# Strassen's scheme for the gate products of two feed-forward stages

## The chip, the core and the metric

The kernel runs on one core of a Trainium2 chip. The metric is the device time of one execution in microseconds (us). Engines: TensorE (PE; its weight loads are shown apart, as PEld), VectorE (DVE), ScalarE (ACT), GpSimd (POOL) and SyncE (SP, which here issues DMAs).

## What is computed

A sequence of 512 tokens with 1024 features goes through two blocks in float32: a convolution mixer and a dilated attention mixer, each with a gated projection behind it; then a feed-forward stage, a mixer (sparse attention and an mLSTM), and a second feed-forward stage. The change touches the two feed-forward stages alone:

```python
def swiglu_ffn(x, g, w_gate, w_up, w_down):   # x (1, 512, 1024), w_gate, w_up (1024, 2816), w_down (2816, 1024)
    h = rms_norm_2(x, g)
    return (jax.nn.silu(h @ w_gate) * (h @ w_up)) @ w_down
...
x = x + 0.5 * swiglu_ffn(x, ...)
```

## The kernel before

Activations lie transposed, features on the 128 partitions and the 512 tokens along the row: x is eight tiles of 128x512 (k.xT). All large products are made in three passes: each operand is split into a high part (rounded to the type fp32r, which TensorE takes) and a low part (the rest), and mm3 (line 216) issues high x high, high x low and low x high into one PSUM bank. Each of the three matmuls loads its own 128x128 weights.

Weights come through one stream (class Stream, line 54) in a fixed order of *granules*, mostly 512 KB, written down in weight_specs. load (line 64) issues a granule's DMA from SP into one of 4 raw buffers (RBUFS). split (line 73) makes the high part on ScalarE (line 85) and the low part on VectorE, or on GpSimd for granules whose number is in POOL_LO (line 87); both halves have 6 buffers (WBUFS). fill keeps six granules split ahead of the first that is still in use; done notes that a granule is used up and lets fill run a few ticks later (a tick is one call of mm3).

A feed-forward stage (ffn, line 1453) has 22 inner tiles of 128 features. For each, a_tile takes the gate granule ("fg") and the up granule ("fu"): eight blocks of 128 input features, 24 matmuls of 512 columns each, into one PSUM bank. The input is split without the norm's factor, so e1 multiplies gate and up by the factor nm.rB out of PSUM on VectorE, with silu on ScalarE between; e2 multiplies the two and splits the product. The first two tiles run as one group of four banks, and half-way through it the norm's statistics are made (Norm.stats, with a power on GpSimd, line 213). The down product is made in parts of 8, 8 and 6 inner tiles (FFN_PARTS): after the first tile of the next part, down (line 1481) runs eight output tiles over the part's inner tiles, and out adds each to k.xT (line 1489). ffn_order (line 430) writes this order, ffn_specs (line 443) the granules that it takes. Arena (line 116) hands out 71 tiles of SBUF and 8 PSUM banks.

The order of the work on each engine is the order of these calls, but for a scheduler that places instructions by its own estimate of when they can run; generators added by add_side are advanced a little at every tick.

Of the kernel before, what the change touches and what calls it, by code (L numbers as in the profile page):

```python
# [11 lines left out]
F32 = mybir.dt.float32  # L12
F32R = mybir.dt.float32r
I32 = mybir.dt.int32
AF = mybir.ActivationFunctionType
OP = mybir.AluOpType
# [7 lines left out]
GRAN = 1024  # L24
WBUFS = 6
FILL = 3
UNITS = ('aq', 'mx', 'mo', 'mv')
POOL_KEYS = ()
# [5 lines left out]
POOL_LO = (0, 1, 2, 3, 4, 5) + tuple(range(24, 37))  # L34
RBUFS = 4
# [9 lines left out]
def gran(key, w, k0, nk, *cols):  # L45

    pieces, off = [], 0
    for c0, n in cols:
        pieces.append((off, n, w[k0 * 128:(k0 + nk) * 128, c0:c0 + n].rearrange("(k p) c -> p k c", p=128)))
        off += n  # L50
    return key, nk, off, pieces


class Stream:
# [3 lines left out]
    def __init__(self, k, pool, specs):  # L58
        self.k, self.pool, self.specs = k, pool, specs
        self.raw, self.parts, self.held = {}, {}, set()  # L60
        self.nd = self.ns = self.pos = 0
        self.hold, self.due = False, None

    def load(self):
        i = self.nd
        self.nd += 1
        t = self.pool.tile([128, GRAN], F32, tag="raw", name="raw", bufs=RBUFS)
        _, nk, width, pieces = self.specs[i]
        for off, n, src in pieces:
            self.k.nc.sync.dma_start(t[:, :nk * width].rearrange("p (k c) -> p k c", k=nk)[:, :, off:off + n], src)  # L70
        self.raw[i] = t

    def split(self):
        i = self.ns
        while self.nd <= min(i + RBUFS - 1, len(self.specs) - 1):
            self.load()
        self.ns += 1
        n = self.specs[i][1] * self.specs[i][2]
        raw = self.raw.pop(i)
        hi = self.pool.tile([128, GRAN], F32R, tag="whi", name="whi", bufs=WBUFS)  # L80
        lo = self.pool.tile([128, GRAN], F32R, tag="wlo", name="wlo", bufs=WBUFS)
        with ExitStack() as ctx:
            if self.k.behind is not None:
                ctx.enter_context(self.k.tc.issue_after(self.k.behind.ins))
            self.last_hi = self.k.nc.scalar.activation(hi[:, :n], raw[:, :n], AF.Copy)  # L85
            eng = self.k.nc.gpsimd if i in POOL_LO or self.specs[i][0][0] in POOL_KEYS else self.k.nc.vector
            eng.tensor_tensor(lo[:, :n], raw[:, :n], hi[:, :n].bitcast(F32), OP.subtract)  # L87
        self.parts[i] = (hi, lo)

    def fill(self, limit=None):  # L90
        first = min(self.held) if self.held else self.pos
# [12 lines left out]
    def done(self, i):  # L104
        self.held.discard(i)
        self.parts.pop(i)
        if self.due is None:
            self.due = self.k.t + FILL
# [170 lines left out]
class Norm:  # L279
# [9 lines left out]
    def add(self, x):  # L289
        k, nc = self.k, self.k.nc  # L290
        hi, lo = k.mem.get(F32R), k.mem.get(F32R)
        g = k.col(self.gain, self.at + self.n)
        sq = k.mem.get()
        nc.scalar.activation(hi, x, AF.Copy, scale=g)
        nc.scalar.activation(sq, x, AF.Square)
        self.finish()
        self.open = (x, hi, lo, g, sq)
        self.n += 1
# [77 lines left out]
def weight_specs(a):  # L376
# [18 lines left out]
    for n in range(4):  # L395
        sp.append(gran(("ao", n), a["attn_w_out"][0], 0, 4, (256 * n, 256)))
    ple_specs(sp, a, 1)
    ffn_specs(sp, a, 1)
    w = a["w_in_2"][0]
    for n in range(4):  # L400
# [15 lines left out]
    for n in range(8):  # L416
        sp.append(gran(("wo", n), a["w_out_2"][0], 0, 8, (128 * n, 128)))
    ffn_specs(sp, a, 2)
    return sp

# [3 lines left out]
        sp.append(gran((key, j), w, 2 * j, 2, (c0, 512)))  # L424


FFN_PARTS = (8, 8, 6)


def ffn_order():  # L430

    order, k0 = [], 0
    for p, n in enumerate(FFN_PARTS):
        for i in range(n):
            order.append(("up", k0 + i))
            if p and i == 0:
                order.append(("down", p - 1))
        k0 += n
    order.append(("down", len(FFN_PARTS) - 1))
    return order  # L440


def ffn_specs(sp, a, l):
    wg, wu, wd = (a[f"ffn{l}_w_{n}_2"][0] for n in ("gate", "up", "down"))
    for what, i in ffn_order():
        if what == "up":
            sp.append(gran(("fg", l, i), wg, 0, 8, (128 * i, 128)))
            sp.append(gran(("fu", l, i), wu, 0, 8, (128 * i, 128)))
        else:
            for m in range(8):  # L450
                sp.append(gran(("fd", l, i, m), wd, sum(FFN_PARTS[:i]), FFN_PARTS[i], (128 * m, 128)))


def pp_specs(sp, a, l):
# [24 lines left out]
def vectors(k, load_x):  # L479
# [31 lines left out]
    def rest():  # L511
# [7 lines left out]
        k.mem.put(pr, dr)  # L519

    load(0, 1)
    load_x()
    for _ in range(3):
        k.W.load()
    dw = a["conv_dw"][0].rearrange("t (c f) -> (t c) f", f=128)
    nc.sync.dma_start(dr[:124, 0:128], dw[0:124])
    nc.sync.dma_start(dr[:124, 128:256], dw[124:248])
    load(1, len(parts))
    return first, rest

# [922 lines left out]
def ffn(k, l, nm, done):  # L1453

    nc, mem, ps_ = k.nc, k.mem, k.ps
    V = nc.vector
    X, H, T = nm.X, {}, {}
    order = ffn_order()
    starts = [sum(FFN_PARTS[:p]) for p in range(len(FFN_PARTS))]
    count = 0  # L1460
    queue = deque()

    def e1(i, pg, pu):
        a, b = mem.get(), mem.get()
        V.tensor_tensor(a, pg, nm.rB, OP.mult)  # L1465
        ps_.put(pg)
        nc.scalar.activation(a, a, AF.Silu)
        V.tensor_tensor(b, pu, nm.rB, OP.mult)  # L1468
        ps_.put(pu)
        queue.append((i, a, b))  # L1470
        while len(queue) > 1:
            e2()

    def e2():
        i, a, b = queue.popleft()
        V.tensor_tensor(a, a, b, OP.mult)  # L1476
        mem.put(b)
        H[i] = k.split_into(a)
        mem.put(a)

    def down(p):
        n, k0 = FFN_PARTS[p], starts[p]
        last = p == len(FFN_PARTS) - 1
        while queue and queue[0][0] < k0 + n:
            e2()
        Hs = [H.pop(k0 + i) for i in range(n)]

        def out(m, ps):
            V.scalar_tensor_tensor(k.xT[m], ps, 0.5, k.xT[m], OP.mult, OP.add)  # L1489
            ps_.put(ps)  # L1490
            if last:
                done(m)
        m0 = 0
        if last:
            m0 = 4
            pss = k.a_group(Hs, [("fd", l, p, m) for m in range(4)])
            for m in range(4):
                out(m, pss[m])
        for m in range(m0, 8):
            out(m, k.a_tile(Hs, ("fd", l, p, m)))  # L1500
        for h, lo in Hs:
            mem.put(h, lo)

    i = 0
    while i < len(order):
        what, j = order[i]
        if what == "down":
            if j == len(FFN_PARTS) - 1:
                for h, lo in nm.X:
                    mem.put(h, lo)  # L1510
            down(j)
        elif i == 0:
            p4 = k.a_group(X, [("fg", l, 0), ("fu", l, 0), ("fg", l, 1), ("fu", l, 1)], nm.stats)
            k.defer(0, lambda: e1(0, p4[0], p4[1]))
            k.defer(0, lambda: e1(1, p4[2], p4[3]))
            i += 1
        else:
            pg = k.a_tile(X, ("fg", l, j))
            pu = k.a_tile(X, ("fu", l, j))
            k.after(lambda j=j, pg=pg, pu=pu: e1(j, pg, pu))  # L1520
        i += 1
    mem.put(nm.rB)

# [532 lines left out]
@with_exitstack  # L2058
def body(ctx, tc, *args):
    a = dict(zip(_INS, args[:-1]))  # L2060
    k = Kern(ctx, tc, a, args[-1])
    k.W = Stream(k, k.wp, weight_specs(a))
    nm, pp = layer0(k)
    nm1 = Norm(k, "norm", 8, keep=True)
    ple(k, 0, nm, pp, nm1)
    nm, pp = layer1(k, nm1)
    nm3 = Norm(k, "ffn1")
    ple(k, 1, nm, pp, nm3)
    nm4 = Norm(k, "mix")
    ffn(k, 1, nm3, lambda m: nm4.add(k.xT[m]))  # L2070
    nm4.finish()
    nm5 = Norm(k, "ffn2")
    mixer(k, nm4, nm5)
    ffn(k, 2, nm5, store(k))
    k.flush()
# [27 lines left out]
```

## Time and profile before

| | |
|---|---|
| median of 3 runs | 1829.97 us (1829.23 to 1831.29) |
| profiled execution | 1830.0 us, span 1828.0 us, mean granted TensorE clock 0.991 |
| TensorE busy in the span | 1793.0 us (98%), 8316 matmuls |
| VectorE, ScalarE, GpSimd busy | 1074.1, 805.8, 257.1 us |
| mean DMA rate | 89 GB/s |

The span runs from the first to the last instruction. Matmuls are pipelined and their ends are modelled: the printed duration of one is longer than the step from its start to the next one's, and the step is what a sequence of them costs. L12 is line 12 of the kernel; tiles are named by their program names: b is a PSUM bank, s a tile of the arena, whi and wlo the weights' high and low parts, raw a granule as loaded.

### The profile page before, as it was taken

To read this page: it belongs to the slowest core of one execution; us is meant where nothing else is said; L and a number is where in the kernel's file an instruction comes from. 1 tells how busy PE (TensorE), PEld (TensorE's weight loads), DVE (VectorE), ACT (ScalarE), POOL (GpSimd) and SP (SyncE) were. 2 spreads that over 40 slices of the span, in tenths; PEclk is the share of its full clock that TensorE was granted. 3 is DMA by queue.
4 is the path that set the end of the run, shared out by engine and by line. 5 is a ranking of instruction groups with operands and counts; after the bars stand their busy time and mean duration, and the time that the engine had idled before them with its cause. 6 is when DMAs were issued, how large, how long until landed. Compare 5 with 4: busy or idle time off the path is not lost. (4 is left out here: it accounts for less than half of the span.)

```text
span 1828.0 us, 21884 instructions
## 1 busy us (share of the span) xinstructions
PE 1793.0 (98%) x8316; PEld 1459.3 (80%) x8316; DVE 1074.1 (59%) x2064; ACT 805.8 (44%) x1345; POOL 257.1 (14%) x210
## 2 busy tenths in 40 slices
PE   7998899999999999999999999899999999999999
PEld 6876688888888888888888887778888888888887
DVE  6989667755466665434433559997446554344342
ACT  6776535465556443222212436567632333122221
POOL 4999210302120000000000001000000000000000
PEclk9999899999999999999999999899999999999999
DMA  6322133212322233333332432013232333333321
GB/s 191 112 81 81 47 93 116 70 53 84 97 85 67 81 93 86 97 94 92 93 92 79 133 113 87 24 52 89 68 125 83 93 104 93 93 94 100 95 70 46
DMA packets 262484, 161.91 MB, mean 89 GB/s; under 512 B 10000, under 2 KB 244844, under 8 KB 262380
## 3 DMA queue, kind: packets, MB, share of 16 engines
q1 hardware_dynamic: 262380, 160.53, 30.2%
q8 instruction: 65, 1.06, 0.2%
q14 instruction: 39, 0.32, 0.1%
HBM read 155.23 MB, written 5.28 MB: 88 GB/s over the span
## 5 line engine op out<-in xcount | busy, mean ns | idle before, releaser
L219 PE MATMUL b<-s,whi 128*128 128x512 f32 x1856 | 740.9, 399 | 0.2
L218 PE MATMUL b<-s,whi 128*128 128x512 f32 x1856 | 737.8, 400 | 3.2 <-ACT s L563 2.2
L220 PE MATMUL b<-s,wlo 128*128 128x512 f32 x1856 | 738.8, 398 | 0.0
L85 ACT ACTIVATE whi<-raw 128x1024 fp32r<-128x1024 f32 (+2 forms) x288 | 297.4, 1041 | 683.1 <-PE b L219 440.9
L218 PEld LDWEIGHTS b<-s,whi 128*128 128x128 f32 x1856 | 350.4, 189 | 88.5 <-ACT s L563 2.6
L219 PEld LDWEIGHTS b<-s,whi 128*128 128x128 f32 x1856 | 351.0, 189 | 86.5 <-issue 2.4
L220 PEld LDWEIGHTS b<-s,wlo 128*128 128x128 f32 x1856 | 350.1, 189 | 83.1 <-issue 1.2
L87 DVE TENSOR_TENSOR wlo<-raw,whi 128x1024 fp32r<-128x1024 f32 (+2 forms) x269 | 331.1, 1234 | 57.2 <-ACT whi L85 50.7
L218 PE MATMUL b<-whi,s 128*128 128x512 f32 (+1 forms) x416 | 172.5, 416 | 0.2 <-DVE s L1772 0.2
L219 PE MATMUL b<-wlo,s 128*128 128x512 f32 (+1 forms) x416 | 168.9, 406 | 0.0
L220 PE MATMUL b<-whi,s 128*128 128x512 f32 (+1 forms) x416 | 165.1, 397 | 0.0
L642 POOL TENSOR_TENSOR s<-s,s 128x512 f32<-128x512 f32 x88 | 128.2, 1488 | 3.4 <-ACT s L638 2.2
L1489 DVE SCALAR_TENSOR_TENSOR s<-b,s 128x512 f32<-128x512 f32 x48 | 33.1, 691 | 144.7 <-PE b L220 144.6
L1468 DVE TENSOR_TENSOR s<-b,s 128x512 f32<-128x512 f32 x44 | 30.4, 691 | 138.4 <-PE b L220 138.4
L644 DVE SCALAR_TENSOR_TENSOR b<-s,s,b 128x512 f32<-128x512 f32 x144 | 99.9, 747 | 3.6 <-ACT b L632 2.9
L220 PEld LDWEIGHTS b<-whi,s 128*128 128x128 f32 x416 | 79.2, 190 | 13.8
L218 PEld LDWEIGHTS b<-whi,s 128*128 128x128 f32 x416 | 79.3, 191 | 12.7 <-DVE s L1772 0.3
L219 PEld LDWEIGHTS b<-wlo,s 128*128 128x128 f32 x416 | 79.3, 191 | 11.0
L1465 DVE TENSOR_TENSOR s<-b,s 128x512 f32<-128x512 f32 x44 | 30.4, 691 | 93.3 <-PE b L220 93.3
L638 ACT ACTIVATE s<-s,s 128x512 f32<-128x512 f32 x96 | 66.2, 717 | 35.0 <-POOL s L642 34.9
L213 POOL TENSOR_TENSOR h8y<-hv,mhalf 128x8 f32<-128x8 f32 x28 | 47.4, 1694 | 131.4 <-DVE hv L1001 113.9
L232 ACT ACTIVATE s<-s 128x512 fp32r<-128x512 f32 x56 | 35.3, 631 | 42.3 <-DVE s L1476 31.8
(417 smaller groups left out, 1698.9 us busy)
## 6 DMA issues: line engine op xcount, KB each, us to landing
raw<-in_ffn_w_gate SPq DMA_DIRECT2D x44, 512.0 KB
raw<-in_ffn_w_up SPq DMA_DIRECT2D x44, 512.0 KB
raw<-in_attn_w_in SPq DMA_DIRECT2D x40, 512.0 KB
raw<-in_w_in SPq DMA_DIRECT2D x36, 512.0 KB
raw<-in_ffn_w_down SPq DMA_DIRECT2D x32, 512.0 KB
raw<-in_conv_w_in SPq DMA_DIRECT2D x24, 512.0 KB
raw<-in_ple_w_gate SPq DMA_DIRECT2D x16, 512.0 KB
raw<-in_ffn_w_down SPq DMA_DIRECT2D x16, 384.0 KB
```

The costliest lines, as they stand in the source:

```text
L85: self.last_hi = self.k.nc.scalar.activation(hi[:, :n], raw[:, :n], AF.Copy)
L87: eng.tensor_tensor(lo[:, :n], raw[:, :n], hi[:, :n].bitcast(F32), OP.subtract)
L213: self.nc.gpsimd.tensor_tensor(y, v, self.mhalf[:, :shape], OP.pow)
L218: mm(ps, a[0], b[0], start=first, stop=False)
L219: mm(ps, a[0], b[1], start=False, stop=False)
L220: self.last = mm(ps, a[1], b[0], start=False, stop=last)
L232: i = nc.scalar.activation(hi, src, AF.Copy)
L638: k.tap = nc.scalar.activation(p, y[:, nd + sent:nd + sent + S], AF.Copy, scale=wcol(nd + sent, c))
L642: nc.gpsimd.tensor_tensor(acc2, acc2, p, OP.add)
L644: nc.vector.scalar_tensor_tensor(acc, y[:, t:t + S], wcol(t, c), acc, OP.mult, OP.add)
L1465: V.tensor_tensor(a, pg, nm.rB, OP.mult)
L1489: V.scalar_tensor_tensor(k.xT[m], ps, 0.5, k.xT[m], OP.mult, OP.add)
```

## The change

In each stage the first 6 inner tiles stay as they are (FFN_PLAIN), and the other 16 go in eight pairs. For a pair, the gate product is seen as a 2x2 block product: the weights of two inner tiles (two columns) by two halves of the 1024 input features (two rows), and the input by two halves of the features and two halves of the tokens. Strassen's scheme, in Winograd's form, makes it from seven products of half-size blocks instead of eight, with sums of blocks on both sides and combinations of the products.

- The input: turn_x, a side generator in the time of tiles 2 to 5, multiplies x by the norm's gain and factor, forms the sums t1 to t4 and splits blocks and sums; turn_rest makes the last eight splits inside the first pair. The result is 16 split tiles (TX) per stage, in place of nm.X.
- The weights: a pair takes four "fs" granules (split_sums): the first gate tile as it is; two sums; two sums; the rest of the second tile. Two are loaded, the other two are made of the same raw buffers, which stay in use longer. VectorE makes four sums of 512 columns per pair.
- The products (two): seven products of 4 blocks x 3 passes, each for 256 tokens, so 256 columns per matmul and two products to a bank. The up products of the pair take the same token halves, also in matmuls of 256 columns.
- The combinations: first, second and third add the products out of PSUM on VectorE in seven operations of 256 columns. The norm's factor is already in, so the multiplications by rB are gone for these tiles.
- FFN_PARTS becomes (6, 4, 6, 6), so the down product has four parts a stage and 64 granules in both stages instead of 48.
- The low parts of the gate and up granules from tile 2 on, of all down granules, and of the first and last "fs" granule of a pair move from VectorE to GpSimd (POOL_MORE, halves).

```diff
@@ class Stream
     def split(self):
         i = self.ns
-        while self.nd <= min(i + RBUFS - 1, len(self.specs) - 1):
+        while self.nd < len(self.specs) and (self.live < RBUFS or not self.specs[self.nd][3]):
             self.load()
...
+        if key[0] == "fs":
+            return self.split_sums(i, key[3])
...
+    def halves(self, parts, cols, src, pool=False):
+        hi, lo = (t[:, cols] for t in parts)
...
+            self.last_hi = self.k.nc.scalar.activation(hi, src, AF.Copy)
+            eng = self.k.nc.gpsimd if pool else self.k.nc.vector
+            eng.tensor_tensor(lo, src, hi.bitcast(F32), OP.subtract)
+
+    def split_sums(self, i, j):
+        V, mem = self.k.nc.vector, self.k.mem
+        one, two = slice(0, 512), slice(512, 1024)
+        p = self.parts[i] = self.two()
+        if j == 0:
+            A = self.blk["a"] = self.raw.pop(i)
+            self.halves(p, slice(0, 1024), A, True)
+        elif j == 1:
+            B = self.blk["b"] = self.raw.pop(i)
+            A = self.blk["a"]
+            s1, s2 = mem.get(), mem.get()
+            V.tensor_tensor(s1, B[:, one], B[:, two], OP.add)
+            V.tensor_tensor(s2, s1, A[:, one], OP.subtract)
+            self.halves(p, two, s2)
+            self.halves(p, one, s1)
...
+        elif j == 2:
+            A, B, s2 = self.blk.pop("a"), self.blk["b"], self.blk.pop("s")
+            s3 = mem.get()
+            V.tensor_tensor(s3, A[:, one], B[:, one], OP.subtract)
+            V.tensor_tensor(s2, A[:, two], s2, OP.subtract)
+            self.live -= 1
+            self.halves(p, one, s3)
+            self.halves(p, two, s2)
...
+        else:
+            self.halves(p, one, self.blk.pop("b")[:, two], True)
+            self.live -= 1
@@
-FFN_PARTS = (8, 8, 6)
+FFN_PARTS = (6, 4, 6, 6)
+FFN_PLAIN = 6
@@ def ffn_specs
+        elif what == "two":
+            for j in range(2):
+                sp.append(gran(("fs", l, i, j), wg, 0, 8, (128 * (i + j), 128)))
+            sp.append(gran(("fu", l, i), wu, 0, 8, (128 * i, 128)))
+            for j in (2, 3):
+                sp.append((("fs", l, i, j), 8, 128, []))
+            sp.append(gran(("fu", l, i + 1), wu, 0, 8, (128 * (i + 1), 128)))
...
+POOL_MORE = {(n, l, i) for n in ("fg", "fu") for l in (1, 2) for i in range(2, 22)}
+POOL_MORE |= {("fd", l, p, m) for l in (1, 2) for p in range(len(FFN_PARTS)) for m in range(8)}
@@ def ffn
+    def turn_x():
...
+        for j in range(2):
+            q = {}
+            for kh in range(2):
+                for th in range(2):
+                    t = q[kh, th] = mem.get()
+                    for e in range(2):
+                        n = 4 * kh + 2 * j + e
+                        V.scalar_tensor_tensor(t[:, e * 256:(e + 1) * 256], k.xT[n][:, th * 256:(th + 1) * 256],
+                                               k.col(nm.gain, nm.at + n), nm.rB[:, th * 256:(th + 1) * 256],
+                                               OP.mult, OP.mult)
...
+            V.tensor_tensor(t1, b12, b11, OP.subtract)
+            V.tensor_tensor(t2, b22, t1, OP.subtract)
...
+            for name, t in (("t2", t2), ("t1", t1)):
+                TX[name, j] = k.split_into(t)
...
+        def product(ps, th, e, off, name):
...
+            for kk in range(4):
+                c = slice(off + kk * 128, off + kk * 128 + 128)
+                b = [t[:, halves2[kk % 2]] for t in TX[name, kk // 2]]
+                k.mm3(ps[:, halves2[th]], (hi[:, c], lo[:, c]), b, kk == 0, kk == 3)
...
+        def plain(i):
...
+            for th in range(2):
+                for kk in range(8):
+                    b = [t[:, halves2[kk % 2]] for t in TX[("b11", "b12", "b21", "b22")[kk // 4 * 2 + th], kk % 4 // 2]]
+                    k.mm3(ps[:, halves2[th]], k.wpart(g, kk * 128), b, kk == 0, kk == 7)
...
+        product(x, 0, 0, 0, "b11")
+        product(x, 1, 0, 512, "b21")
+        k.W.done(gs[0])
+        if wait:
+            turn_rest()
+        product(y, 0, 1, 512, "t2")
+        product(y, 1, 1, 0, "t1")
+        k.W.done(gs[1])
+        def first():
+            nc.scalar.activation(p1, x[:, L], AF.Copy)
+            add(a0[:, L], x[:, R], p1)
+            ps_.put(x)
+            add(u2, y[:, L], p1)
+            add(u4, y[:, R], u2)
+        k.after(first)
+        pu0 = plain(i0)
+        z, w = ps_.get(), ps_.get()
+        product(z, 0, 2, 0, "t3")
+        product(z, 1, 2, 512, "b22")
+        k.W.done(gs[2])
+        def second():
+            add(a0[:, R], z[:, R], u4)
+            add(u3, z[:, L], u2)
+            add(a1[:, R], y[:, R], u3)
+            ps_.put(y, z)
+            nc.scalar.activation(a0, a0, AF.Silu)
+        k.after(second)
+        product(w, 0, 3, 0, "t4")
+        k.W.done(gs[3])
+        def third():
+            add(a1[:, L], u3, w[:, L], OP.subtract)
...
+            nc.scalar.activation(a1, a1, AF.Silu)
+            add(a0, a0, pu0, OP.mult)
+            ps_.put(pu0)
+            H[i0] = k.split_into(a0)
...
+        pu1 = plain(i0 + 1)
+        def end():
+            add(a1, a1, pu1, OP.mult)
+            ps_.put(pu1)
+            H[i0 + 1] = k.split_into(a1)
...
```

## Rows read from the trace of the kernel before

**Rows 1.** The page: busy time, share of the span and instructions of each engine.

```profile
PE 1793.0 (98%) x8316; PEld 1459.3 (80%) x8316; DVE 1074.1 (59%) x2064; ACT 805.8 (44%) x1345; POOL 257.1 (14%) x210
```

**Rows 2.** Windows of both stages: length; PE, PEld, DVE, ACT, POOL busy us; clock; DMA.

```profile
703.00:1072.00 369.00, 369.00 (x1586) 296.79 (x1585) 162.50 (x203) 103.78 (x128) 4.13 (x7) 1.00 0.35 100
1463.00:1826.00 363.00, 360.62 (x1573) 291.25 (x1571) 147.48 (x179) 95.84 (x116) 1.01 (x1) 1.00 0.30 87
```

**Rows 3.** Groups of TensorE, 700 to 1072 us: busy us, mean ns, idle before.

```profile
L218 PE MATMUL b<-s,whi 128*128 128x512 f32 x527 | 208.2, 395 | 0.0
```

**Rows 4.** Timeline of TensorE, 24 steps in each stage: start us, duration us.

```profile
906.06 0.39 PE L218 MATMUL b<-s,whi 128*128 128x512 f32 x1
...
911.69 0.39 PE L218 MATMUL b<-s,whi 128*128 128x512 f32 x1
...
1599.68 0.39 PE L218 MATMUL b<-s,whi 128*128 128x512 f32 x1
...
1605.26 0.39 PE L218 MATMUL b<-s,whi 128*128 128x512 f32 x1
```

**Rows 5.** Timeline of TensorE in the mixer, 1099.77 to 1105.59 us.

```profile
1099.77 0.39 PE L219 MATMUL b<-wlo,s 128*128 128x512 f32 x1
...
1102.80 0.39 PE L220 MATMUL b<-whi,s 128*128 128x512 f32 x1
1103.04 0.64 PE L984 MATMUL b<-s,s 128*128 128x256 f32 x4
1103.51 0.64 PE L985 MATMUL b<-s,s 128*128 128x256 f32 x4
1103.99 0.28 PE L984 MATMUL b<-s,s 128*128 128x256 f32 x1
1104.10 0.29 PE L985 MATMUL b<-s,s 128*128 128x256 f32 x1
...
1104.80 0.37 PE L984 MATMUL b<-s,s 128*128 128x256 f32 x1
1105.00 0.28 PE L985 MATMUL b<-s,s 128*128 128x256 f32 x1
...
1105.59 0.39 PE L218 MATMUL b<-whi,s 128*128 128x512 f32 x1
```

**Rows 6.** Timeline of TensorE, matmuls of 336 columns, 21 steps.

```profile
1086.72 0.31 PE L219 MATMUL b<-wlo,s 128*128 128x336 f32 x1
...
1089.94 0.32 PE L219 MATMUL b<-wlo,s 128*128 128x336 f32 x1
```

**Rows 7.** Groups of VectorE by shape, 760 to 1050 us (first stage).

```profile
L87 DVE TENSOR_TENSOR wlo<-raw,whi 128x1024 fp32r<-128x1024 f32 x45 | 55.0, 1223 | 5.7 <-ACT whi L85 5.7
L1476 DVE TENSOR_TENSOR s<-s,s 128x512 f32<-128x512 f32 x16 | 11.1, 691 | 1.4
```

**Rows 8.** Groups of GpSimd in the whole span: the low part of 1024 columns.

```profile
L87 POOL TENSOR_TENSOR wlo<-raw,whi 128x1024 fp32r<-128x1024 f32 x19 | 46.5, 2458 | 41.2 <-ACT whi L85 41.2
```

**Rows 9.** Groups of ScalarE by shape, 760 to 1050 us.

```profile
L85 ACT ACTIVATE whi<-raw 128x1024 fp32r<-128x1024 f32 x45 | 47.7, 1061 | 164.7 <-PE b L219 116.1 <-issue 48.6
L232 ACT ACTIVATE s<-s 128x512 fp32r<-128x512 f32 x16 | 10.1, 633 | 13.3 <-DVE s L1476 13.3
```

**Rows 10.** VectorE's subtraction, 42 to 140 us, and that window (columns as in rows 2).

```profile
L87 DVE TENSOR_TENSOR wlo<-raw,whi 128x1024 fp32r<-128x1024 f32 x18 | 31.2, 1732 | 6.6 <-ACT whi L85 5.7 <-POOL s L642 1.0
...
42.00:140.00 98.00, 97.31 (x414) 76.84 (x412) 90.11 (x110) 73.60 (x107) 97.14 (x65) 1.00 0.33 97
```

**Rows 11.** Timeline of SP's queue at the start: DMA issues.

```profile
4.97 5.48 SPq L70 DMA_DIRECT2D raw<-in_conv_w_in  x3
```

**Rows 12.** Timeline of ScalarE at the start: the first granules' high parts.

```profile
13.22 2.08 ACT L85 ACTIVATE whi<-raw 128x1024 fp32r<-128x1024 f32 x2
```

**Rows 13.** Line 218, 700 to 1072 us: events on the load queue (ns, min/median/max).

```profile
L218 PEldq EVENT_SEMAPHORE  x1: 51/51/51, 733.3 to 733.3; - x1
```

**Rows 14.** Timeline of weight loads for matmuls of one column, 1463 us.

```profile
1463.03 0.86 PEld L319 LDWEIGHTS b<-ones,s 128*128 128x128 f32 x7
```

## Prediction: what the change does to the time

> **What bounds the kernel now.** I read the page's engine totals first: TensorE is busy 1793.0 of the 1828.0 us span, VectorE 1074.1, ScalarE 805.8 and GpSimd 257.1 [rows 1]. That is an average over unlike stages, so I next cut out the two feed-forward stages by windows [rows 2]. Each is some 370 us long; TensorE fills 369.00 of 369.00 us in one and 360.62 of 363.00 in the other at granted clock 1.00, VectorE is busy 162.50 and 147.48, ScalarE 103.78 and 95.84, GpSimd 4.13 and 1.01, and the DMA engines are at 0.35 and 0.30. In the groups of the first stage the matmuls show no idle time before them [rows 3] (two more groups, of lines 219 and 220, show the same): nothing that VectorE, ScalarE or DMA does there is late. So inside these stages time is the number of matmuls times the step from one matmul's start to the next, and only that. The printed duration of a matmul (395 ns) is not that step, as matmuls overlap; it is read from the starts in the timeline. 24 matmuls of 512 columns, one inner tile's gate or up product, take 906.06 to 911.69 us, 0.2346 us each, in the first stage, and 1599.68 to 1605.26, 0.2325 each, in the second [rows 4]; I use the mean, 0.2335.
>
> **What leaves and comes on TensorE.** A stage has 22 inner tiles. The first 6 stay as they are; 16 go in 8 pairs, so 16 pairs in both stages. Today a pair costs 2 tiles x 2 products (gate, up) x 8 blocks x 3 passes = 96 matmuls of 512 columns: 96 x 0.2335 = 22.42 us. After: seven half-size gate products of 4 blocks x 3 passes, 84 matmuls, and two up products whose 512 columns are now issued as two halves, 2 x 2 x 8 x 3 = 96; all 180 have 256 columns. In columns that is 90 x 512 instead of 96 x 512. Everything therefore hangs on the step of a 256-column matmul that brings its own weight load. The trace has such runs in the mixer: from 1103.04 to 1104.10, and from 1105.00 to 1105.59, 9 and 5 steps, together 1.65 us or 0.1179 each, beside 512-column steps of (1102.80 - 1099.77) / 13 = 0.2331 in the same stretch [rows 5]; the kernel has as many weight loads as matmuls, 8316 [rows 1], one for each. 336 columns step by (1089.94 - 1086.72) / 21 = 0.1533 [rows 6], so 0.456 ns per column at 336 and 0.455 at 512 (0.2331), and 0.461 at 256: nearly in proportion, with about 1 ns fixed. Scaled to the stages' pace, 0.1179 x 0.2335 / 0.2331 = 0.1181. 180 x 0.1181 = 21.26 us, so a pair saves 22.42 - 21.26 = 1.16 us and 16 pairs save **18.5 us**. Bounds of this term: no fixed part at all, 256 x 0.455 = 0.1165, gives 22.42 - 20.97 = 1.45 a pair, 23.2 us; 0.120, somewhat above the second run's 0.59 / 5 = 0.118 and the first eight steps' 0.95 / 8 = 0.119, gives 0.82 a pair, 13.1 us. I keep 18.5, as those rows are the same kind of instruction (one load, one matmul of 256 columns).
>
> The down products change from parts of 8, 8, 6 tiles to 6, 4, 6, 6: the same 22 x 8 x 3 matmuls a stage, no cost on TensorE. The last part still has 6 tiles, so the stage's end and the store behind the second stage stay.
>
> **What comes on the other engines, and its cover.** Cover is the pair's 21.3 us plus its share of the down products, 2 x 8 x 3 x 0.2335 = 11.2 us: 32.5 us.
> VectorE per pair: four sums and four low parts of half granules, 8 x 0.69; seven combinations of 256 columns out of PSUM, bounded by the 0.69 of 512 columns; two multiplications and two low parts of the result, 4 x 0.69; output additions 8/3 x 0.69 [rows 7]. (8 + 7 + 4 + 2.7) x 0.69 = 15.0 of 32.5 us at most. GpSimd, nearly idle here now, takes the low parts of the first gate granule, of a half granule, of two up granules and of 8/3 smaller down granules, none above the 2.46 of 1024 columns [rows 8]: 6.7 x 2.46 = 16.4 of 32.5 at most. ScalarE: one gate and two up granules x 1.06, 8/3 down granules at most as much, five halves and five passes of up to 512 columns x 0.63: 3.2 + 2.8 + 6.3 = 12.3 of 32.5 [rows 9]. Each is near half or under, so I cost them at nothing; if the cover were gone, the price is whatever TensorE waits.
>
> Whether a *chain* is late is another question. Six weight granules are kept ready (WBUFS), and a pair consumes six (two double gate granules 2.8 us each, up 5.7, a third double one 2.8, a single one 1.4, up 5.7), so a granule's buffer comes free one pair ahead of its next use, less its own time: 18.5 us for a 2.8 us granule. The longest chain is the second gate granule's: two sums (1.4), then ScalarE and VectorE on both halves (0.63 + 0.69, partly overlapped), some 4 us. VectorE is slowed by a busy GpSimd: the same 1024-column subtraction takes 1.23 us in the stages now and 1.73 where GpSimd works without pause [rows 7, 10]; 1.4 times 4 us still lies far inside 18.5. The two raw buffers that a pair holds longer (four exist) delay its successor's loads: the second gate tile's next load starts when the sums of the third product are made, and is wanted after one single product, an up and two double ones, 1.4 + 5.7 + 2.8 + 2.8 = 12.7 us later. At the start of the kernel three raw loads issued from 4.97 us were in use by 13.22, 8.3 us [rows 11, 12]; that is the worst landing I find, and it fits. SP only issues loads; none of its other work is moved. GpSimd's queue holds one thing that TensorE comes to wait for, the power of the norm (line 213): it is made half-way through the group of the first two tiles, some 20 x 0.70 us after the low parts of tile 2 are queued and before those of tile 3, so I cost it at nothing; a collision would be 2.5 us a stage, 5 us in all.
> The sums and splits of x (turn_x) are on VectorE at most (16 + 8 + 8) x 0.69 = 22 us before the first pair, spread over tiles 2 to 5 (45 us, in which their own VectorE work is about 11 us now that GpSimd takes the low parts). The remaining eight splits come in one lump of 5 us on ScalarE behind the first two products; the first of them wanted, b12, is needed 2.8 + 2.8 us later and lies first in the lump, the last group at 8.5 us. Cost: nothing, up to 1 us a stage. PSUM: a pair takes six of eight banks and frees two of them before its second half; no wait.
>
> Sum: against the profiled execution, 1830.0 us (span 1828.0 and 2.0 around it, the median of the runs shown being 1829.97): 1830.0 - 18.5 = 1811.5, with a few tenths for the first pair **1812 us**.
>
> **Rivals.**
> *A, part of the gain lost to hand-overs:* a pair has 11 accumulation groups instead of 4. A wait that TensorE's queue takes as an event of its own shows as 51 ns [rows 13], and a run that starts behind a wait has a first step of 0.20 instead of 0.118 (1104.80 to 1105.00 [rows 5]). Seven more groups at 0.05 to 0.09 are 0.36 to 0.6 us a pair, 6 to 10 us: 1817 to 1822. Against: 512-column groups show no such cost, as the line that opens every group has one such event in the whole first stage [rows 13]. 13 in 100. With short stalls on top the gain is gone within what can be told: 1826 to 1834, 5 in 100.
> *B, slower: the weight load isn't hidden behind 256 columns.* Seven loads for matmuls of one column step by (0.86 - 0.19) / 6 = 0.112 us [rows 14]; against 0.1165 for the columns the cover is only 5 ns, where at 512 it is 120. [...] It decides from 22.42 / 180 = 0.1246 up. [...] 7 in 100, 1827 to 1845.
> [...]
> *C, slower: the sums' chain.* If every one of the second gate granule's six VectorE steps waited for a whole GpSimd instruction (0.69 + 2.46 each, plus 1.3 on ScalarE), the chain would be 20 us against 18.5 of lead, TensorE would wait up to 2 us a pair, and 32 us would be added to 1811.5: 1844. It decides from 1.16 us a pair. GpSimd is busy half of the time at most, so this needs every step to collide. 5 in 100.
>
> **How the numbers follow.** The forecast 70, A 13, A with the gain gone 5, B 7, C 5 in 100. Forecast's own range, from the bounds of the step: 1806 to 1817; with A the range of 8 in 10 is 1805 to 1826. This kernel's measurement tells about 0.2%, 3.7 us, from no change: faster is the forecast and nearly all of A, 0.82; same 0.06; slower 0.12.
>
> **What will show it.** Right: 180-matmul pairs with steps of 0.117 to 0.120 us, no idle time before the matmuls of the new lines, stages shorter by 9 us each, GpSimd busy over 200 us more, VectorE no more than 60% in the stages. Wrong: steps of 0.122 or more (B); idle time of TensorE put down to ScalarE, VectorE or GpSimd splits (C) or many events on its load queue (A); a mixer or first half whose time moves, which nothing above allows for.

## The result, and the profile after

The changed kernel takes 1809.86 us (median of 4 runs, 1809.37 to 1814.68) against 1830.08 before; the ratio is 0.9895 with a 95% interval of 0.9877 to 0.9913. The forecast was 1812 in a range of 1805 to 1826, faster. The profiled execution took 1809.8 us, with a span of 1807.9.

The page's totals, the windows of the two stages (columns as in [rows 2]; the stages are now shorter, so the windows are too), and one of TensorE's groups in the first of them (its others show the same 0.0 of idle time):

```profile
PE 1772.4 (98%) x9660; PEld 1509.1 (83%) x9660; DVE 1131.4 (63%) x2208; ACT 859.8 (48%) x1475; POOL 556.1 (31%) x354
```

```profile
703.00:1062.00 359.00, 359.00 (x2254) 322.04 (x2253) 189.37 (x276) 128.99 (x191) 147.23 (x77) 1.00 0.36 103
1451.00:1806.00 355.00, 352.45 (x2247) 317.38 (x2245) 175.51 (x253) 121.40 (x180) 145.14 (x71) 1.00 0.31 89
```

```profile
L264 PE MATMUL b<-s,whi 128*128 128x256 f32 x480 | 134.6, 280 | 0.0
```

There are 1344 more matmuls (9660 for 8316 [rows 1]), which is 16 x 84, and TensorE is as full as before: no idle time before its groups [rows 3], 359.00 of 359.00 us [rows 2]. VectorE, ScalarE and GpSimd work more, and none of it is on the path. The step of a 256-column matmul, which carried the forecast, is now seen over a long run. TensorE's timeline, first and last start of 86 steps:

```profile
811.82 0.28 PE L265 MATMUL b<-s,whi 128*128 128x256 f32 x1
...
821.96 0.28 PE L264 MATMUL b<-s,whi 128*128 128x256 f32 x1
```

10.14 / 86 = 0.1179 us, as in the mixer's short runs [rows 5]. Where the 20 us came from is read from marks that both kernels have on TensorE, in order of time: the statistics ahead of the first stage, the first transposes of the mixer, the norm's spreading in the second stage, and the first transposes of the store. Before:

```profile
646.89 0.83 PE L319 MATMUL b<-ones,s 128*128 128x1 f32 x7
...
1090.10 0.49 PE L1603 MATMUL b<-ident,s 128*128 128x128 f32 x3
...
1469.99 1.05 PE L357 MATMUL b<-diag,ones 128*128 128x128 f32 x8
...
1806.19 1.03 PE L2048 MATMUL b<-ident,s 128*128 128x128 f32 x8
```

After:

```profile
646.16 0.95 PE L365 MATMUL b<-ones,s 128*128 128x1 f32 x8
...
1079.20 0.49 PE L1805 MATMUL b<-ident,s 128*128 128x128 f32 x3
...
1458.46 1.05 PE L403 MATMUL b<-diag,ones 128*128 128x128 f32 x8
...
1786.11 1.91 PE L2250 MATMUL b<-ident,s 128*128 128x128 f32 x16
```

The lead of the changed kernel is 0.73, 10.90, 11.53 and 20.08 us. So the two stages give 10.2 and 8.6 us, 18.7 together; the untouched parts ahead of the first and between them differ by 0.7 and 0.6 between these two executions. Where the size of a loss matters below, the stages are measured between these marks as well, because the part ahead of the first mark moves by some us from one execution to the next (646.16 here, 649.77 in e6_rest12).

### The profile page after: what moved, and what is told of

Its sections match the earlier page's. It is cut to its first block, busy times and chain, and to the rows that moved or that the text cites. A ratio compares the mean times of both kernels' runs of the same rounds, so it can differ in the third digit from the quotient of the medians.

```text
span 1807.9 us, 25187 instructions
## 1 busy us (share of the span) xinstructions
PE 1772.4 (98%) x9660; PEld 1509.1 (83%) x9660; DVE 1131.4 (63%) x2208; ACT 859.8 (48%) x1475; POOL 556.1 (31%) x354
## 5 line engine op out<-in xcount | busy, mean ns | idle before, releaser
L265 PE MATMUL b<-s,whi 128*128 128x512 f32 (+1 forms) x2304 | 807.2, 350 | 0.2
L264 PE MATMUL b<-s,whi 128*128 128x512 f32 (+1 forms) x2304 | 804.8, 351 | 2.5 <-ACT s L625 1.3
L266 PE MATMUL b<-s,wlo 128*128 128x512 f32 (+1 forms) x2304 | 805.1, 350 | 0.0
L100 ACT ACTIVATE whi<-raw 128x1024 fp32r<-128x1024 f32 (+2 forms) x304 | 293.6, 973 | 524.4 <-PE b L265 290.0
L102 POOL TENSOR_TENSOR wlo<-raw,whi 128x1024 fp32r<-128x1024 f32 (+2 forms) x163 | 345.8, 2129 | 549.9 <-ACT whi L100 524.0
L264 PEld LDWEIGHTS b<-s,whi 128*128 128x128 f32 x2304 | 434.7, 189 | 63.9 <-ACT s L862 2.2
L265 PEld LDWEIGHTS b<-s,whi 128*128 128x128 f32 x2304 | 434.9, 189 | 62.7 <-issue 2.2
L266 PEld LDWEIGHTS b<-s,wlo 128*128 128x128 f32 x2304 | 435.2, 189 | 60.7 <-issue 1.2
L102 DVE TENSOR_TENSOR wlo<-raw,whi 128x1024 fp32r<-128x1024 f32 (+1 forms) x141 | 179.3, 1275 | 37.1 <-ACT whi L100 30.8
L1636 DVE TENSOR_TENSOR s<-b,s 128x256 f32<-128x256 f32 x96 | 38.9, 421 | 132.5 <-PE b L266 112.1
L1551 DVE SCALAR_TENSOR_TENSOR s<-b,s 128x512 f32<-128x512 f32 x64 | 44.1, 688 | 107.3 <-PE b L266 107.3
L279 DVE TENSOR_TENSOR s<-s,s 128x512 fp32r<-128x512 f32 x88 | 90.1, 1038 | 31.6 <-ACT s L278 31.5
```

What stands on the lines that cost most here:

```text
L100: self.last_hi = self.k.nc.scalar.activation(hi, src, AF.Copy)
L102: eng.tensor_tensor(lo, src, hi.bitcast(F32), OP.subtract)
L264: mm(ps, a[0], b[0], start=first, stop=False)
L265: mm(ps, a[0], b[1], start=False, stop=False)
L266: self.last = mm(ps, a[1], b[0], start=False, stop=last)
L279: nc.vector.tensor_tensor(lo, src, hi.bitcast(F32), OP.subtract)
```

## Experiments

The theory: inside the two stages the time is the sum of TensorE's steps, a step goes with the columns and hardly with the number of matmuls, and the new work elsewhere is hidden. Times below stand against the kernel before on the same chip, 1830.7 to 1830.9 us; the changed kernel's own ratio is 0.9895.

### Halving the matmuls alone (e1_halves)

```diff
+    def a_tile2(self, X, key):
...
+        for th in range(2):
+            c = slice(256 * th, 256 * th + 256)
+            for j in range(8):
+                self.mm3(ps[:, c], self.wpart(g, j * 128), [t[:, c] for t in X[j]], j == 0, j == 7)
...
-            pg = k.a_tile(X, ("fg", l, j))
-            pu = k.a_tile(X, ("fu", l, j))
+            tile = k.a_tile2 if j >= 6 else k.a_tile
+            pg = tile(X, ("fg", l, j))
+            pu = tile(X, ("fu", l, j))
```

> The kernel before, in which only the 16 later inner tiles of each stage issue their gate and up products as two halves of 256 columns (192 matmuls a pair instead of 96; no sums, no seven products, no moved work). The theory that a step is proportional to columns with about 1 ns fixed gives 192 x 0.1180 = 22.66 us a pair against 22.42, so 16 x 0.24 = +4 us: 1833 to 1835. [...] The rival in which groups of matmuls pay 0.05 to 0.09 us for a hand-over gives up to 4 more groups a pair, +3 to +6 us on top.

Measured: 1834.29 us, ratio 1.0025 (1.0014 to 1.0036), against 1830.94 of the same runs: +3.4 us by the medians, +4.6 by the ratio and +5.1 between the marks, about the 4 us of the theory. 16 x 96 = 1536 more matmuls, each with its weight load, cost 2 to 3 ns apiece. A step of 0.1246 us, from which rival B decides, would have cost 16 x (192 x 0.1246 - 22.42) = 24 us, and hand-overs 3 to 6 us more. With it the rest of the gain is named as well: against this kernel the seven products save 24 us, of which 16 pairs x 12 matmuls x 0.118 = 22.7 us are the eighth product that is no longer made.

### The side edits alone (e2_moves)

```diff
-FFN_PARTS = (8, 8, 6)
+FFN_PARTS = (6, 4, 6, 6)
...
-            eng = self.k.nc.gpsimd if i in POOL_LO or self.specs[i][0][0] in POOL_KEYS else self.k.nc.vector
+            key = self.specs[i][0]
+            eng = self.k.nc.gpsimd if i in POOL_LO or key[0] in POOL_KEYS or key in POOL_MORE else self.k.nc.vector
```

> The kernel before with two side edits of the change alone: down parts 6, 4, 6, 6 and the low parts of the later gate and up granules and of all down granules on GpSimd. No product is changed. The theory that only the number of matmuls counts gives no change, 1829 to 1831. The rival that part of the 20 us came from relieving VectorE or from the smaller down parts gives 1820 or less; the rival that these edits cost something which the seven products had to win back gives 1834 or more.

Measured: 1830.53 us, ratio 0.9998 (0.9989 to 1.0007). No part of the gain comes from the smaller down parts or from VectorE's relief, although GpSimd took over some 146 us of work in the first stage (150.25 busy here, 4.13 before [rows 2]). The windows of this kernel:

```profile
703.00:1072.00 369.00, 369.00 (x1586) 296.87 (x1586) 134.38 (x146) 104.93 (x137) 150.25 (x76) 1.00 0.35 99
```

VectorE falls from 162.50 [rows 2] to 134.38 us, and the same 1586 matmuls of TensorE fall into the same 369 us.

### The low parts back on VectorE (e3_no_pool)

```diff
+POOL_MORE = set()
...
-            self.halves(p, slice(0, 1024), A, True)
+            self.halves(p, slice(0, 1024), A)
...
-            self.halves(p, one, self.blk.pop("b")[:, two], True)
+            self.halves(p, one, self.blk.pop("b")[:, two])
```

> The changed kernel with all low parts that it moved to GpSimd back on VectorE. VectorE then works about 22 to 24 of the 32.5 us of a pair and its down share, GpSimd nothing. The theory that cover is ample gives the time of the changed kernel, 1809 to 1811. The rival that the sums' chain needs GpSimd's help, or that VectorE comes late for PSUM, gives waits of TensorE, 1815 or more; the rival that VectorE and GpSimd getting into each other's way costs time in the changed kernel gives 1807 or less.

Measured: 1810.72 us, ratio 0.9896 (0.9882 to 0.9910), the changed kernel's. So the move to GpSimd, too, brings nothing here. VectorE then works 219.76 us of the first stage instead of 189.37. In the changed kernel GpSimd's work holds VectorE up, and that costs no time either: VectorE's low parts of the results, in the changed kernel and in this one, 775 to 1040 us (busy us, mean ns):

```profile
L279 DVE TENSOR_TENSOR s<-s,s 128x512 fp32r<-128x512 f32 x14 | 21.3, 1519 | 9.6 <-ACT s L278 9.6
```

```profile
L279 DVE TENSOR_TENSOR s<-s,s 128x512 fp32r<-128x512 f32 x14 | 9.6, 688 | 0.4
```

### A longer chain of sums (e4_sums7)

```diff
-            V.tensor_tensor(s1, B[:, one], B[:, two], OP.add)
+            for _ in range(7):
+                V.tensor_tensor(s1, B[:, one], B[:, two], OP.add)
```

> The changed kernel with the first weight sum of each pair made seven times over, six additions of 512 columns more, 4.1 us in the chain of the second gate granule. The theory (lead 18.5 us, chain 4 to 8 us) gives no change, 1809 to 1811. The rival that the chain is almost late gives 16 x up to 4 us, 1815 to 1870.

Measured: 1814.43 us, ratio 0.9914 (0.9900 to 0.9929), 3.7 us over e3_no_pool, which ran beside it. The 95% intervals of the two ratios just overlap; between the marks (646.14, 1080.49, 1458.51 and 1788.24 here) the stages are 1.3 and 2.1 us longer than in the changed kernel, 3.4 together. Neither expectation holds: there is a loss, but not in every pair. TensorE has three stretches of waiting in the two stages, and all of them are in the first pair, in its first up product. What ended them stands in brackets, one in the first stage and two in the second:

```profile
762.19 0.28 PE L265 MATMUL b<-s,whi 128*128 128x256 f32 x1
763.46 0.39 PE L266 MATMUL b<-s,whi 128*128 128x256 f32 x1 [0.99 <-DVE s L280]
...
1515.73 0.39 PE L266 MATMUL b<-s,whi 128*128 128x256 f32 x1 [0.34 <-DVE s L280]
...
1522.74 0.38 PE L266 MATMUL b<-s,whi 128*128 128x256 f32 x1 [1.01 <-DVE s L280]
```

Line 280 of that kernel is the low part in split_to: the last splits of x (turn_rest), which are queued on VectorE behind the weight sums of that same pair. VectorE's timeline, in the changed kernel and in e4_sums7:

```profile
755.44 0.69 DVE L1538 TENSOR_TENSOR s<-s,s 128x512 f32<-128x512 f32 x1
756.04 1.89 DVE L279 TENSOR_TENSOR s<-s,s 128x512 fp32r<-128x512 f32 x3
```

```profile
759.91 2.89 DVE L1539 TENSOR_TENSOR s<-s,s 128x512 f32<-128x512 f32 x1
762.73 1.88 DVE L280 TENSOR_TENSOR s<-s,s 128x512 fp32r<-128x512 f32 x3
```

TensorE's next matmul was due at 762.3, one step behind 762.19, and starts at 763.46, when the first of the last three splits is done. In the changed kernel that one ends at about 756.7, so it has some 5.5 us to spare. In e4_sums7 it comes 6.7 us later: VectorE is 4.5 us behind when it comes to these splits, of which six sums of 0.69 are 4.1, and 2.2 more come from line 1539 (line 1538 in the changed kernel), which takes 2.89 instead of 0.69 us there.

### The added sums in the first pair alone (e5_first6)

```diff
+        key = self.specs[i][0]
...
-            V.tensor_tensor(s1, B[:, one], B[:, two], OP.add)
+            for _ in range(7 if key[2] == FFN_PLAIN else 1):
+                V.tensor_tensor(s1, B[:, one], B[:, two], OP.add)
```

> The changed kernel with the first weight sum made seven times over in the first pair of each stage only. The theory formed from the run before (the thin place is the last splits of x in the first pair, which stand behind the sums on VectorE) puts the whole loss of the seven-fold sums here: 3 to 4 us over the changed kernel, 1813 to 1815, with TensorE waiting for a split of x once or a few times near the first pair's up product. The rival (the weight sums' own chain is near late in every pair) gives an eighth of it, under 1 us.

Measured: 1815.35 us, ratio 0.9912 (0.9897 to 0.9927). That is a little above the 1813 to 1815 that I expected, but between the marks (650.21, 1084.57, 1462.72 and 1792.46) the stages lose the same 1.3 and 2.1 us as in e4_sums7, with the same one wait in the first stage and two in the second, again for a split of x. The whole loss is here, and the new theory holds for this spot.

### Twelve more sums in all pairs but the first (e6_rest12)

```diff
+            for _ in range(1 if key[2] == FFN_PLAIN else 13):
+                V.tensor_tensor(s1, B[:, one], B[:, two], OP.add)
```

> The changed kernel with the first weight sum made thirteen times over in all pairs but the first, 8.3 us more in the chain of the second gate granule and on VectorE, which then works about 25 of 32.5 us. The theory (lead 18.5 us, chain 4 + 8.3 = 12.3 us) gives no change, 1809 to 1811. The rival (chain near late) gives 14 pairs x 1 to 8 us, 1824 or more.

Measured: 1825.61 us, ratio 0.9965 (0.9954 to 0.9976). That is 15.8 us over the changed kernel's median where I expected none. The time lies in the rival's range, but not by its mechanism: between the marks (649.77, 1089.03, 1467.98 and 1801.89) the stages are 6.2 and 6.3 us longer, 12.5 together (most of the rest stands ahead of the first mark, where the two kernels don't differ), and this is lost at four places and not at fourteen: two pairs in each stage, the second and third of three pairs in a row without down products between them. TensorE there:

```profile
895.33 0.28 PE L268 MATMUL b<-s,wlo 128*128 128x256 f32 x1
897.02 0.39 PE L266 MATMUL b<-s,whi 128*128 128x256 f32 x1 [1.42 <-ACT whi L100]
897.26 0.28 PE L267 MATMUL b<-s,whi 128*128 128x256 f32 x1
898.17 0.39 PE L268 MATMUL b<-s,wlo 128*128 128x256 f32 x1 [0.63 <-DVE wlo L102]
...
899.30 0.41 PE L268 MATMUL b<-s,wlo 128*128 128x256 f32 x1
899.52 0.41 PE L266 MATMUL b<-s,whi 128*128 128x256 f32 x1
```

SP's loads and VectorE's sums (line 119) that led to it:

```profile
876.15 0.99 SPq L73 DMA_DIRECT2D raw<-in_ffn_w_gate  x2
```

```profile
873.30 2.78 DVE L129 TENSOR_TENSOR s<-raw,s 128x512 f32<-128x512 f32 x1
...
881.94 2.36 DVE L119 TENSOR_TENSOR s<-raw 128x512 f32<-128x512 f32 x1
...
894.90 0.68 DVE L119 TENSOR_TENSOR s<-raw 128x512 f32<-128x512 f32 x1
```

The next pair's gate tiles are loaded at 876.15, when the previous pair's last sum (line 129) has let go of a raw buffer. Their first sum starts at 881.94, and TensorE wants the result at 895.45. So the chain has 13.5 us here, not the 18.5 of the split weights' buffers; it took 13.6 us to the end of the first sums alone, 13 x 0.69 = 9.0 stretched by the combinations and one sum of the third granule that VectorE makes between them, and by the 2.36 us of its first one. In the changed kernel, without the added sums in the pair before, this same pair's chain has 25.1 us, and the shortest of the eight in the first stage has 19.4 (851.24 to 870.62). The pair's first sum there, which waits for the DMA, and TensorE's first matmul with the result:

```profile
866.73 0.79 DVE L117 TENSOR_TENSOR s<-raw 128x512 f32<-128x512 f32 x1 [0.87 <-DMA raw<-in_ffn_w_gate]
```

```profile
891.83 0.28 PE L264 MATMUL b<-s,whi 128*128 128x256 f32 x1
```

### The same with five raw buffers (e8_raw5), and five alone (e9_after_raw5)

```diff
-RBUFS = 4
+RBUFS = 5
...
-SLOTS = 71
+SLOTS = 70
```

> The kernel with the thirteen-fold sums in all pairs but the first, and five raw buffers instead of four (and one arena tile fewer). If the lead that ran out there is that of the raw buffers (the second gate tile's next load stands behind the previous pair's sums, so a chain has 13 us from landing to use, not 18.5), the load goes out before those sums and the loss of 15 us over the changed kernel shrinks to 0 to 3 us: 1809 to 1813. If the lead is that of the split weights' buffers, or VectorE is simply too full, the time stays at 1820 or more.

> The changed kernel with five raw buffers and one arena tile fewer, nothing else. Both theories give the time of the changed kernel, 1809 to 1811, as no weight is late there; a lower time would mean that loads do cost something in the changed kernel.

Measured: e8_raw5 1814.16 us, ratio 0.9908 (0.9893 to 0.9923); e9_after_raw5, the changed kernel with the fifth buffer alone, 1809.86, ratio 0.9884 (0.9867 to 0.9900). With one more buffer the loss falls from 15.8 to 4.3 us at the same work on VectorE, so what ran out in e6_rest12 was mostly the raw buffers' lead. 4.3 us by the medians is more than the 0 to 3 I had written; between the marks (648.95, 1083.00, 1461.39 and 1790.39) the stages lose 1.0 and 1.4 us, 2.4 together. Of the two places in each stage one is left: the third of the three pairs still waits, the second no longer does. What limits the third isn't settled. In the changed kernel itself the fifth buffer is worth nothing.

### Both products by the scheme (e7_both)

The up products of the same pairs get the same seven products. The four granules are made by the same split_sums; one more low part per product goes to GpSimd; the last splits of x are issued at the start of the first pair, and b12, which no product needs any more, isn't split.

```diff
-            sp.append(gran(("fu", l, i), wu, 0, 8, (128 * i, 128)))
             for j in (2, 3):
                 sp.append((("fs", l, i, j), 8, 128, []))
-            sp.append(gran(("fu", l, i + 1), wu, 0, 8, (128 * (i + 1), 128)))
+            for j in range(2):
+                sp.append(gran(("us", l, i, j), wu, 0, 8, (128 * (i + j), 128)))
+            for j in (2, 3):
+                sp.append((("us", l, i, j), 8, 128, []))
...
-            self.halves(p, one, s1)
+            self.halves(p, one, s1, True)
...
-        pu0 = plain(i0)
...
-        pu1 = plain(i0 + 1)
...
+        g = strassen("fs", True, None)
...
+        strassen("us", False, last)
```

> The changed kernel with the up products of the same pairs by the same seven products too, so 168 matmuls of 256 columns a pair instead of 180; VectorE makes eight weight sums and fourteen combinations a pair, one more quarter of the low parts goes to GpSimd. The theory that TensorE's matmul count sets the time gives 16 x 12 x 0.118 = 22.7 us less than the changed kernel, 1787 to 1789. The rival that VectorE, then at some 25 of 31 us and held up by GpSimd, comes late gives waits of TensorE and 1792 or more; in the first pair, where splits of x now have 3 us less lead, a few us of wait may show in any case.

Measured: 1787.82 us, ratio 0.9762 (0.9747 to 0.9777): 22 us less than the changed kernel, 16 x 12 x 0.118 = 22.7 being the matmuls left out. The window of its first stage:

```profile
703.00:1050.00 347.00, 347.00 (x2159) 310.47 (x2158) 254.32 (x379) 146.37 (x232) 168.69 (x93) 1.00 0.37 106
```

VectorE now works 73% of the stage, and TensorE still never waits. This version beats both kernels.

## Why the prediction was right

- **The bound.** That the stages are TensorE's steps and nothing else holds: e2_moves and e3_no_pool put some 145 us of GpSimd's work into a stage or take it out and leave the time where it was; e1_halves and e7_both change the number of matmuls, and the time follows the columns but for 2 to 3 ns a matmul.
- **The step.** 0.1181 forecast, 0.1179 measured; this term carried the sum. Its bounds, 0.1165 and 0.120, were far wider than needed. The fixed part, forecast as about 1 ns from three lengths, is 2 to 3 ns by e1_halves.
- **The sum.** 18.5 us forecast, 20.2 measured (20.1 between the spans of the two profiled executions). Between the marks the two stages give 18.7, so the sum itself was nearly exact; most of the rest, 1.4 us, is the parts that the change doesn't touch; it lies within what executions differ by and is chance. By stage 9.25 each was expected, and 10.2 and 8.6 came: the forecast used one mean step for both stages, and with each stage's own, 0.2346 and 0.2325 [rows 4], 768 steps less 1440 of 0.1179 give 10.4 and 8.8. In the second stage the 512-column matmuls that remain step by (1483.36 - 1477.76) / 24 = 0.2333, where before the sampled tile had 0.2325 [rows 4]; why the step there was shorter before is open.

```profile
1477.76 0.40 PE L264 MATMUL b<-s,whi 128*128 128x512 f32 x1
...
1483.36 0.40 PE L264 MATMUL b<-s,whi 128*128 128x512 f32 x1
```

- **Rival A, hand-overs.** The events are there and cost nothing. On line 264, 703 to 1062 us, the load queue has 47 for 1 before [rows 13], and the step is 0.118 all the same; so the 51 ns of an event on that queue weren't 51 ns of TensorE here. The first step of 0.20 us that the forecast put down to a wait follows one of 0.03 in the kernel before (1104.77 to 1104.80), with no idle time ahead of it; together they are 0.23, the sum of a 128-column step of 0.11 and a 256-column step of 0.118, so nothing was lost there. Behind the waits of e4_sums7 and e6_rest12 the first step was 0.23 and 0.24 us (763.46 to 763.69, 897.02 to 897.26); in the changed kernel's two stages TensorE has no such wait. No step between two 256-column matmuls of the first stage is over 0.124 us, so nothing like the 0.05 to 0.09 us of a hand-over is there:

```profile
L264 PEldq EVENT_SEMAPHORE  x47: 51/51/51, 721.3 to 1037.1; - x47
```

- **Rival B, exposed loads.** Excluded: the step is 0.118 us in 86 steps in a row as in nine, where a loss begins at 0.1246, so the 5 ns of cover that I feared were thin are enough. Its range, 1827 to 1845, was my estimate: no run shows a fixed part that would lead there; e1_halves shows 2 to 3 ns a matmul in its place.
- **Rival C, the sums' chain.** No wait in the changed kernel, as forecast, and 18.5 us was not too much for the lead there: the 16 chains have 19.3 to 29.9 us from the first sum to use. What the forecast lacked is that this lead isn't fixed. The raw buffer that gates the load is let go by the previous pair's sums, so longer chains make the next one late: with 8.3 us more in each, 13.5 us are left (e6_rest12), and a fifth buffer gives most of it back (e8_raw5). The forecast had this second lead in hand, but as 12.7 us for the load alone, and did not add the chain to the landing; with its 8.3 us of landing and 4 of chain that would have been nearly full. It isn't, because the sums are made well ahead of the product that takes them: the second gate tile of the pair that starts at 889 us is loaded from 862.93 on, 28.9 us before its use.
- **The first pair.** "Cost: nothing, up to 1 us a stage" was right in the time and weak in the reason: the place with the least cover that these runs found is there, some 5.5 us for the last splits of x (e4_sums7, e5_first6); the pairs' weights have 19 us or more for a chain that I put at 4.

## What to carry to other kernels

Where TensorE is full and its loads are hidden, price a rearranged product by columns, from the start-to-start step of the nearest rows of the same width; in these runs one matmul more cost 2 to 3 ns, down to 256 columns. For work that is moved on to other engines, busy shares answer only half of the question: follow each chain through *every* buffer that gates its start, the raw one as well as the finished one, ask whether the added work itself delays the release of that buffer, and look first at the one-time set-up, which had less cover here than the loop. Adding work until the time moves tells how much cover there is, and where.

## What the runs showed of the hardware

VectorE's subtractions were longer beside GpSimd's. In the changed kernel it makes 14 low parts of 512 columns on line 279 from 775 to 1040 us. Nine of them began 0.5 to 0.8 us into a low part of GpSimd; they took 1.03 to 2.47 us, and each ended 0.55 us after that low part. The other five took 0.69 us: four had no GpSimd instruction beside them, one began 0.05 us before a low part ended. One of the nine:

```profile
825.84 2.47 DVE L279 TENSOR_TENSOR s<-s,s 128x512 fp32r<-128x512 f32 x1 [0.85 <-ACT s L278]
```

```profile
825.36 2.40 POOL L102 TENSOR_TENSOR wlo<-raw,whi 128x1024 fp32r<-128x1024 f32 x1 [4.63 <-ACT whi L100]
```

The forecast had a factor of 1.4 from [rows 10], which is a mean: single ones of those 18 took 1.23 to 2.26 us.

In e6_rest12 TensorE lost more than the length of its waits. Behind the two at 895 to 898 us the 256-column step rose from 0.118 to 0.213 us and stayed there until 902; the granted clock is 0.57 from 898 to 902 us and 1.00 in the windows before and after. The windows (PE, PEld, DVE, ACT, POOL; then the clock):

```profile
890.00:898.00 8.00, 6.12 (x50) 5.69 (x48) 7.86 (x15) 4.15 (x7) 0.00 (x1) 1.00 0.00 0
898.00:902.00 4.00, 3.83 (x19) 3.83 (x20) 3.97 (x3) 2.54 (x4) 4.00 (x2) 0.57 0.00 0
902.00:910.00 8.00, 8.00 (x70) 8.00 (x69) 7.48 (x8) 1.97 (x3) 5.28 (x3) 1.00 1.01 265
```

Some 17 steps at 0.213 are 1.6 us on top of 2.4 us of waiting. It happened at two of the four places; behind the other two, with waits about half a microsecond shorter (in the first stage 0.9 us against 1.4 for the high part), the step was 0.118 again at once.
